# Scores of the later attention layers as three products of split operands, with the queries held by token tile

## The chip, the cores and the metric

One core of one Trainium2 chip runs the whole program. The metric is the device time of one execution in microseconds (us); the time before is the median of three executions, 2535.29 us (2534.57 to 2535.4).

## What is computed

Two transformer blocks in a row on 256 tokens of width 1024, batch 1. The first has two layers with a second stream of 256 context tokens (differential and neighbourhood attention, then grouped attention over context and tokens). The second has four layers: attention (layer 0), a linear recurrence (1), latent attention (2), attention (3), and in each a cross attention to a memory and a feed-forward part with a short convolution. The change is in the attention of layers 0 and 3 of the second block; the same function also serves the last layer of the first block. Cut to its core, the reference of layers 0 and 3 is

```python
qkv = x @ w_qkv
q, k, v = jnp.split(qkv, ...)
q = apply_rope_2(q.reshape(bsz, s, A_HEADS, A_HEAD_DIM), cos, sin)
k = apply_rope_2(k.reshape(bsz, s, A_KV_HEADS, A_HEAD_DIM), cos, sin)
...
scores = jnp.einsum('bnqhgd,bnkhd->bnhgqk', qb, kb).astype(jnp.float32) * (A_HEAD_DIM ** -0.5)
scores = jnp.where(valid[None, :, None, None], scores, NEG)
probs = jax.nn.softmax(jnp.concatenate([scores, sink], axis=-1), axis=-1)[..., :-1]
out = jnp.einsum('bnhgqk,bnkhd->bnqhgd', probs.astype(v.dtype), vb)
return out.reshape(bsz, s, A_HEADS * A_HEAD_DIM) @ w_o
```

with 16 query heads of width 64, 4 key heads and blocks of 128 tokens: a query of the first token tile sees the 128 keys of its tile, one of the second tile sees 256 keys, through a mask.

## The kernel before, in words

All activations and weights are float32. Large products are made with operands split in two: `split` (L154 to L161) writes a high part, rounded to the type float32r, on ACT, and then on DVE the rest, the low part; `mm3` (L137 to L141) issues three matmuls into the same bank: high by high (L139), one high by the other's low (L140), low by high (L141). `weights` (L125 to L135) loads 1 MB of weights and splits it in four pieces of 512 columns on ACT (L133) and DVE (L134). A product of plain float32 operands is one matmul call, which the trace shows as two records, each with its own weight load.

`gqa` (L675 to L787) makes one attention layer. In layers 0 and 3 (no `cT`) it projects keys and values (`rows`), applies the rotation (`rope`, DVE, last instruction L276), transposes the keys on TensorE (L165) into one PSUM bank `t` and copies them into the tile `kT`, float32, 2 x 256 columns. `query(J)` projects half of the heads, rotates and transposes each token tile (four transposes into bank `t`) and copies it with the factor 0.125 into its columns of `qT`, a float32 tile of 4 x 256 columns in two buffers. `attend` then calls `quad_attn` (L790 to L828) for each half J (2), token tile t (2) and pair of head columns g (2): 8 calls in a layer, 16 in the two layers. A call makes the scores of four heads: for i and j in 0, 1 one matmul (L804) with 64 rows, j being the half of the partitions (0 to 63 or 64 to 127), into the bank `s[j]`:

```python
for i in range(2):
    for j in range(2):
        hs = slice(HD * j, HD * (j + 1))
        nc.tensor.matmul(s[j][:, i * nk : (i + 1) * nk], qT[hs, g + i, t * P : (t + 1) * P], kT[hs, J, :nk],
                         start=True, stop=True)
```

`nk` is 128 for t = 0 and 256 for t = 1. Mask and maximum follow on DVE (L808), the exponentials on ACT (L812), the division on DVE (L818), then four transposes into bank `t` (L165), a copy on ACT (L824), and the products with the values (L826). Bank `t` is a single buffer; `s` has two.

In the last layer of the first block (`cT` given) keys and queries are already split; `pair_attn` (L420 to L462) issues the three products of one half of the partitions, then the three of the other, with 512 columns each.

`copy` (L143 to L152) puts a copy on DVE (L148, L150) or on ACT (L152) by a toggle, `flip`, that every call turns: in layers 0 and 3 the values (2 calls), `kT` (1), `qT` (4) and the 12 copies of `quad_attn`, which turn the toggle too though they are fixed to ACT. The latent attention of layer 2 uses `copy` for its operands (`kr`, `mv`, `qr`, `qk`, `mpt`).

What sets the order: the source lists the instructions, and a scheduler in the tile framework orders them for each engine when the program is built, so that PE works on other matmuls (the next projection, the output projection of `project`, L831 to L861) between the steps of an attention. Semaphores hold an instruction until its operands are there. Each layer's tiles live in a pool of its own (`atM0`, `atM3`).

Of the kernel before, what the change touches and what calls it, by code (L numbers as in the profile page):

```python
# [19 lines left out]
P = 128  # L20
D = 1024
S = 256
# [36 lines left out]
class Net:  # L59
# [615 lines left out]
    def gqa(self, xT, w_qkv, kind, sink, cT=None):  # L675

        nc = self.nc
        T = lambda n, shape, b=1: self.at.tile(shape, F32, tag=n, name=n, bufs=b)
        TT = lambda n, shape, b=1: [self.at.tile(shape, F32R, tag=n + c, name=n + c, bufs=b) for c in "hl"]
        nkt = 4 if cT is not None else 2  # L680
        kT, v = (T if cT is None else TT)("kT", [P, 2, nkt * P]), T("gv", [P, nkt, S])
        oT = self.pair("T", S)
        kv = [self.bank("a") for _ in range(2)]
        if cT is not None:
# [1 line left out]
        def rows(ps, w, kh, t, x=xT):  # L686
            for k in range(4):
                kk = 4 * kh + k
                self.mm3(ps[t], [z[:, kk, t * P : (t + 1) * P] for z in x], [z[:, k, :] for z in w],
                         kk == 0, kk == KD - 1)  # L690
# [26 lines left out]
        pt = self.bank("t")  # L717
# [5 lines left out]
                o = J * S + t * P  # L723
                self.transpose(pt[:, o : o + P], rk[:, J * P : (J + 1) * P])
        pt = pt.rearrange("p (f t) -> p f t", f=2)
        if cT is None:
            self.copy(kT, pt)
        else:
            self.split(pt, *(x[:, :, :S] for x in kT))

        def query(J):
            ps = [self.bank("a") for _ in range(2)]
            for kh in range(2):
                w = [x.rearrange("p (k n) -> p k n", k=4) for x in self.weights(w_qkv[1 + J, kh])]
                for t in range(2):
                    rows(ps, w, kh, t)
            qT = (T if cT is None else TT)("qT", [P, 4, S], 2)
            for t in range(2):
                rq = self.wk.tile([P, 512], F32, tag="w", bufs=4, name="rq")
                self.rope(rq, ps[t], 512, kind, t)  # L740
                pt = self.bank("t")
                for g in range(4):
                    self.transpose(pt[:, g * P : (g + 1) * P], rq[:, g * P : (g + 1) * P])
                pt, ts = pt.rearrange("p (g q) -> p g q", g=4), slice(t * P, (t + 1) * P)
                if cT is None:
                    self.copy(qT[:, :, ts], pt, 0.125)
                else:
                    self.split(pt, *(x[:, :, ts] for x in qT), scale=0.125)
            return qT

        def attend(J, qT, ts=(0, 1)):
            hs = lambda j: slice(HD * j, HD * (j + 1))
            for t in ts:
                ops = self.bank("o")
                ts = slice(t * P, (t + 1) * P)
                if cT is not None:
                    for g in range(4):
                        if t == 0:
                            bias = lambda j: (P, self.cst[:, C_MLE0 : C_MLE0 + P])
                        else:  # L760
                            bias = lambda j: (0, self.cst[:, C_GE0 : C_GE0 + P])
                        self.pair_attn(
                            lambda j: [x[hs(j), g, ts] for x in qT],
                            lambda j: [x[hs(j), J, :] for x in kT],
                            512,
                            lambda j, kb: v[:, kb, (2 * J + j) * HD : (2 * J + j + 1) * HD],
                            ops[:, g * P : (g + 1) * P],
                            bias=bias,
                            sink=sink + 8 * J + 2 * g,
                        )  # L770
                        self.fill(1 if J else g % 2)
                else:
                    for g in range(0, 4, 2):
                        self.quad_attn(qT, kT, v, J, t, g, ops, sink + 8 * J + 2 * g)
                self.split(ops.rearrange("p (g q) -> p g q", g=4), *(o[:, 4 * J : 4 * J + 4, ts] for o in oT))

        q0 = query(0)
        self.update()
        attend(0, q0)
        q1 = query(1)  # L780
        if cT is not None:
            attend(1, q1)
            yield oT, [0, 1, 2, 3]
        else:
            attend(1, q1, (0,))
            yield oT, [0, 1]
            attend(1, q1, (1,))  # L787
            yield oT, [2, 3]

    def quad_attn(self, qT, kT, v, J, t, g, ops, sink):  # L790

        nc = self.nc
        nk = (t + 1) * P
# [6 lines left out]
        s = [self.bank("s") for _ in range(2)]  # L800
        for i in range(2):
            for j in range(2):
                hs = slice(HD * j, HD * (j + 1))
                nc.tensor.matmul(s[j][:, i * nk : (i + 1) * nk], qT[hs, g + i, t * P : (t + 1) * P], kT[hs, J, :nk],  # L804
                                 start=True, stop=True)
        for h in range(4):
            j, i = divmod(h, 2)
            nc.vector.tensor_tensor_reduce(out=e[:, h, :nk], in0=s[j][:, i * nk : (i + 1) * nk], in1=mask, scale=1.0,  # L808
# [10 lines left out]
        for kb in range(t + 1):  # L819
            ps = self.bank("t")  # L820
            pt = self.at.tile([P, 512], F32, tag="pt", name="pt")
# [3 lines left out]
            for j in range(2):  # L825
                nc.tensor.matmul(ops[HD * j : HD * (j + 1), g * P : (g + 2) * P],  # L826
                                 v[:, kb, (2 * J + j) * HD : (2 * J + j + 1) * HD], pt[:, j * S : (j + 1) * S],
                                 start=kb == 0, stop=kb == t, skip_group_check=True)  # L828
# [821 lines left out]
```

## Time and profile before

| | |
|---|---|
| median of three executions | 2535.29 us |
| the profiled execution, its own time | 2532.55 us |
| its span, first to last instruction | 2530.8 us |
| PE busy | 2468.3 us (98%) |
| DVE busy | 1701.7 us (67%) |
| ACT busy | 1214.9 us (48%) |
| granted TensorE clock, mean | 0.996 |

PE is the engine of the matmuls, PEld its weight loads (they overlap PE), DVE the vector engine, ACT the scalar engine. A matmul's record is longer than its share of the engine, since matmuls are pipelined: what one costs is read from start to start. Columns of the timeline: start and duration in us, engine, line, operation, out<-in, shape, how many were merged, and in brackets the idle time before it and what ended it. In the two attention layers the scores lie at 1153 to 1191 us and at 2207 to 2247 us of the span.

### The profile page before, as it was taken

Reading aid. Unit: us, or ns where it says so; the run is one execution under the profiler, and the core shown is the slowest. Engines: PE = TensorE matmul, PEld = TensorE weight load, DVE = VectorE, ACT = ScalarE, POOL = GpSimd, SP = SyncE. Lnnn points to the kernel's source line nnn. Section 1 sums busy time; section 2 is a strip of 40 time slices with the busy share of each in tenths; the row PEclk is TensorE's granted clock in tenths of the full one; section 3 lists DMA queues with packets and bytes.
Section 4 is the critical chain, followed back from the end, with each engine's and each line's share of the span. In section 5 each row is a group of like instructions: output and inputs, shape, how many; then the busy total and the mean of one; then the engine's idle time right before and its main releaser. Section 6 shows DMA issues by size and latency. Waiting matters only on the chain.

```text
span 2530.8 us, 39873 instructions
## 1 busy us (share of the span) xinstructions
PE 2468.3 (98%) x15706; PEld 2094.4 (83%) x15706; DVE 1701.7 (67%) x3602; ACT 1214.9 (48%) x2630; POOL 130.6 (5%) x172
## 2 busy tenths in 40 slices
PE   7999999999999999999999999999999999999998
PEld 5957668777788679986899988999878999869998
DVE  5463674343448765568787789677877777986777
ACT  4242353222235445446455665465555455564664
POOL 2000001111100000000000010000000000000000
PEclk9999999999999999999999999999999999999999
DMA  9415324343223546543545545355345455433643
GB/s 391 171 48 214 124 77 178 138 156 142 89 84 134 212 152 223 192 167 133 183 167 189 189 150 219 125 212 195 135 154 184 149 200 184 169 147 123 236 176 116
DMA packets 63708, 419.31 MB, mean 166 GB/s; under 512 B 7440, under 2 KB 7696, under 8 KB 16928
## 3 DMA queue, kind: packets, MB, share of 16 engines
q1 hardware_dynamic: 62240, 412.56, 45.3%
q0 software_dynamic: 1280, 4.20, 0.5%
q8 instruction: 123, 2.02, 0.3%
q14 instruction: 65, 0.53, 0.1%
HBM read 411.45 MB, written 5.28 MB: 165 GB/s over the span
## 4 chain that ended last, share of the span: by engine, by line
PE 85%; DVE 8%; ACT 3%; issue 1%; POOL 1%; DMA 1%; POOLq 0%; DVEq 0%; ACTq 0%
PE banka L139 9%; PE banka L140 9%; PE banka L141 9%; PE banks L139 6%; PE banks L141 6%; PE banks L140 6%; PE bankb L141 5%; PE bankb L140 5%; PE bankb L139 5%; PE bankt L165 3%; PE banko L141 2%; PE banko L139 2%; PE banko L140 2%; DVE wlo L134 2%; PE bankt L141 2%; PE bankt L140 2%
## 5 line engine op out<-in xcount | busy, mean ns | idle before, releaser
L134 DVE TENSOR_TENSOR wlo<-raw,whi 128x512 fp32r<-128x512 f32 (+1 forms) x1184 | 783.4, 689 | 290.9 <-ACT whi L133 288.1
L133 ACT ACTIVATE whi<-raw 128x512 fp32r<-128x512 f32 (+1 forms) x1184 | 662.7, 620 | 641.0 <-issue 175.4
L141 PE MATMUL banks<-Th,wlo 128*128 128x256 f32 x880 | 249.5, 284 | 3.0 <-DVE wlo L134 3.0
L139 PE MATMUL banks<-Th,whi 128*128 128x256 f32 x880 | 249.3, 283 | 0.6 <-DVE uf L250 0.6
L140 PE MATMUL banks<-Tl,whi 128*128 128x256 f32 x880 | 249.1, 283 | 0.0
L141 PEld LDWEIGHTS banks<-Th,wlo 128*128 128x128 f32 x880 | 168.8, 192 | 4.1 <-DVE wlo L134 4.1
L139 PEld LDWEIGHTS banks<-Th,whi 128*128 128x128 f32 x880 | 168.8, 192 | 1.7 <-issue 0.7
L140 PEld LDWEIGHTS banks<-Tl,whi 128*128 128x128 f32 x880 | 168.8, 192 | 0.8
L139 PE MATMUL banka<-whi,Th 128*128 128x512 f32 (+1 forms) x304 | 122.2, 404 | 2.6 <-ACT Th L157 2.1
L140 PE MATMUL banka<-wlo,Th 128*128 128x512 f32 (+1 forms) x304 | 120.0, 397 | 2.1 <-DVE wlo L134 2.0
L141 PE MATMUL banko<-Th,wlo 128*128 128x256 f32 x424 | 120.9, 285 | 1.1 <-DVE wlo L134 1.1
L655 DVE TENSOR_TENSOR sg<-sg,bankb 128x512 f32<-128x512 f32 x22 | 15.1, 688 | 158.3 <-PE bankb L141 158.3
L139 PE MATMUL bankt<-Th,whi 128*128 128x256 f32 x424 | 120.3, 284 | 0.0
L139 PE MATMUL banko<-Th,whi 128*128 128x256 f32 x424 | 120.1, 283 | 0.0
L141 PE MATMUL bankt<-Th,wlo 128*128 128x256 f32 x424 | 120.0, 283 | 0.0
L140 PE MATMUL bankt<-Tl,whi 128*128 128x256 f32 x424 | 120.0, 283 | 0.0
L140 PE MATMUL banko<-Tl,whi 128*128 128x256 f32 x424 | 119.9, 283 | 0.0
L141 PE MATMUL banka<-whi,Tl 128*128 128x512 f32 (+1 forms) x304 | 117.7, 394 | 0.3 <-DVE Tl L158 0.3
L139 PE MATMUL bankb<-Th,whi 128*128 128x256 f32 (+1 forms) x344 | 115.0, 335 | 0.0
L141 PE MATMUL bankb<-Th,wlo 128*128 128x256 f32 (+1 forms) x344 | 114.8, 334 | 0.0
L140 PE MATMUL bankb<-Tl,whi 128*128 128x256 f32 (+1 forms) x344 | 114.2, 332 | 0.0
L157 ACT ACTIVATE hh<-hf 128x256 fp32r<-128x256 f32 x110 | 45.7, 415 | 135.1 <-DVE hf L955 134.6
(489 smaller groups left out, 6356.2 us busy)
## 6 DMA issues: line engine op xcount, KB each, us to landing
raw<-in_f_w_up_dram SPq DMA_DIRECT2D x88, 1024.0 KB, 4.8
raw<-in_ffn_w_dram SPq DMA_DIRECT2D x66, 1024.0 KB, 4.9
adaw<-in_ada_w_dram SPq DMA_DIRECT2D x48, 1024.0 KB, 4.8
raw<-in_f_w_down_dram SPq DMA_DIRECT2D x44, 1024.0 KB, 5.0
raw<-in_x_w_q_dram SPq DMA_DIRECT2D x16, 1024.0 KB, 4.8
raw<-in_x_w_o_dram SPq DMA_DIRECT2D x16, 1024.0 KB, 5.7
raw<-in_w_in_ab_dram SPq DMA_DIRECT2D x12, 1024.0 KB, 5.8
raw<-in_a_w_qkv_dram SPq DMA_DIRECT2D x12, 1024.0 KB, 4.9
```

The source lines that it names most:

```text
L133: nc.scalar.activation(hi[:, a:b], r[:, a:b], AF.Copy)
L134: nc.vector.tensor_tensor(lo[:, a:b], r[:, a:b], hi[:, a:b].bitcast(F32), op=ALU.subtract)
L139: mm(out, l[0], r[0], start=start, stop=False)
L140: mm(out, l[0], r[1], start=False, stop=False)
L141: mm(out, l[1], r[0], start=False, stop=stop)
L157: nc.scalar.activation(hi, src, AF.Copy)
L165: self.nc.tensor.transpose(out, src, self.ident[:k, :k])
L655: nc.vector.tensor_tensor(sg, sg, ps[1], op=ALU.mult)
```

## The change

In layers 0 and 3 `kT` becomes a pair (high and low, float32r), written by `split` instead of `copy`. `qT` becomes one pair for each token tile, 4 x 128 columns, in three buffers for layers 0 and 3 and in four for the first block's last layer, written by `split` with the factor 0.125. `quad_attn` takes the pair of its token tile and calls `mm3` in place of the one float32 matmul. Five calls of `copy` leave each of layers 0 and 3.

```diff
@@ -678,7 +678,7 @@
-        kT, v = (T if cT is None else TT)("kT", [P, 2, nkt * P]), T("gv", [P, nkt, S])
+        kT, v = TT("kT", [P, 2, nkt * P]), T("gv", [P, nkt, S])
@@ -723,10 +723,7 @@
-        if cT is None:
-            self.copy(kT, pt)
-        else:
-            self.split(pt, *(x[:, :, :S] for x in kT))
+        self.split(pt, *(x[:, :, :S] for x in kT))
@@ -734,18 +731,14 @@
-            qT = (T if cT is None else TT)("qT", [P, 4, S], 2)
+            qT = [TT("qT", [P, 4, P], 3 if cT is None else 4) for _ in range(2)]
...
-                pt, ts = pt.rearrange("p (g q) -> p g q", g=4), slice(t * P, (t + 1) * P)
-                if cT is None:
-                    self.copy(qT[:, :, ts], pt, 0.125)
-                else:
-                    self.split(pt, *(x[:, :, ts] for x in qT), scale=0.125)
+                self.split(pt.rearrange("p (g q) -> p g q", g=4), *qT[t], scale=0.125)
@@ -760,7 +753,7 @@
-                            lambda j: [x[hs(j), g, ts] for x in qT],
+                            lambda j: [x[hs(j), g, :] for x in qT[t]],
@@ -771,7 +764,7 @@
-                        self.quad_attn(qT, kT, v, J, t, g, ops, sink + 8 * J + 2 * g)
+                        self.quad_attn(qT[t], kT, v, J, t, g, ops, sink + 8 * J + 2 * g)
@@ -801,8 +794,8 @@
-                nc.tensor.matmul(s[j][:, i * nk : (i + 1) * nk], qT[hs, g + i, t * P : (t + 1) * P], kT[hs, J, :nk],
-                                 start=True, stop=True)
+                self.mm3(s[j][:, i * nk : (i + 1) * nk], [x[hs, g + i, :] for x in qT], [x[hs, J, :nk] for x in kT],
+                         True, True)
```

## Rows read from the trace of the kernel before

**Rows 1.** The page: busy time by engine, and shares of the chain that ended last.

```profile
PE 2468.3 (98%) x15706; PEld 2094.4 (83%) x15706; DVE 1701.7 (67%) x3602; ACT 1214.9 (48%) x2630; POOL 130.6 (5%) x172
...
PE 85%; DVE 8%; ACT 3%; issue 1%; POOL 1%; DMA 1%; POOLq 0%; DVEq 0%; ACTq 0%
```

**Rows 2.** Windows: stretch, its length, busy us by engine; both attentions, and a full stretch of DVE.

```profile
1150.00:1205.00 55.00, 55.00 (x295) 35.85 (x295) 43.39 (x169) 35.47 (x107) 0.00 (x0) 1.00 0.27 96
2205.00:2260.00 55.00, 54.41 (x294) 35.84 (x293) 44.69 (x172) 35.67 (x107) 0.74 (x2) 1.00 0.30 110
...
2210.00:2220.00 10.00, 10.00 (x56) 6.62 (x55) 9.82 (x44) 7.77 (x25) 0.00 (x0) 1.00 0.57 211
```

**Rows 3.** Groups by line and shape: the score matmuls (busy us, mean ns).

```profile
L804 PE MATMUL banks<-kT,qT 64*128 64x256 f32 x64 | 14.5, 413 | 0.0
L804 PE MATMUL banks<-kT,qT 64*128 64x128 f32 x64 | 6.7, 299 | 0.0
```

**Rows 4.** Timeline of PE: scores of 128 columns, in one stretch and divided.

```profile
1152.44 0.39 PE L141 MATMUL banka<-whi,Tl 128*128 128x512 f32 x1
1152.67 0.40 PE L139 MATMUL banka<-whi,Th 128*128 128x512 f32 x1
1153.00 0.71 PE L804 MATMUL banks<-kT,qT 64*128 64x128 f32 x8
1153.64 0.50 PE L140 MATMUL banka<-wlo,Th 128*128 128x512 f32 x1
...
2209.00 0.49 PE L804 MATMUL banks<-kT,qT 64*128 64x128 f32 x2
```

**Rows 5.** Timeline of PE: scores of 256 columns, in one stretch and divided.

```profile
1156.82 1.14 PE L804 MATMUL banks<-kT,qT 64*128 64x256 f32 x8
...
1161.74 1.13 PE L804 MATMUL banks<-kT,qT 64*128 64x256 f32 x4
...
1163.16 0.70 PE L804 MATMUL banks<-kT,qT 64*128 64x256 f32 x2
```

**Rows 6.** Timeline of PE: split products of 256 columns, one after another.

```profile
1881.14 0.28 PE L139 MATMUL banks<-cqh,whi 128*128 128x256 f32 x1
1881.26 0.28 PE L140 MATMUL banks<-cql,whi 128*128 128x256 f32 x1
```

**Rows 7.** Transposes of 128 columns: four in the timeline, then their group by shape.

```profile
1154.44 0.60 PE L165 MATMUL bankt<-cst,rq 128*128 128x128 f32 x4
...
L165 PE MATMUL bankt<-cst,rq 128*128 128x128 f32 x64 | 10.0, 278 | 2.2 <-DVE rq L276 2.2
```

**Rows 8.** Timeline of PE in the first block's last layer: one pair of split scores.

```profile
870.53 0.50 PE L139 MATMUL banks<-kTh,qTh 64*128 64x512 f32 x1
870.68 0.50 PE L139 MATMUL bankb<-kTh,qTh 64*128 64x512 f32 x1
870.87 0.39 PE L140 MATMUL banks<-kTl,qTh 64*128 64x512 f32 x1
...
871.10 0.39 PE L141 MATMUL banks<-kTh,qTl 64*128 64x512 f32 x1
```

**Rows 9.** Tiles: the copies that go, and the split's two halves (min/median/max ns).

```profile
L152 ACT ACTIVATE qT<-bankt x4: 586/597/599, 1152.2 to 2236.1; 128x512 f32<-128x512 f32 x4
L150 DVE TENSOR_SCALAR qT<-bankt x4: 682/692/692, 1155.1 to 2234.6; 128x512 f32<-128x512 f32 x4
...
L160 ACT ACTIVATE qTh<-bankt x4: 577/589/600, 798.6 to 867.6; 128x512 fp32r<-128x512 f32 x4
L161 DVE SCALAR_TENSOR_TENSOR qTl<-bankt,qTh x4: 681/681/683, 799.4 to 868.4; 128x512 fp32r<-128x512 f32 x4
```

**Rows 10.** Timeline of PE behind the first attention: output projection, first and last of its end.

```profile
1203.99 0.50 PE L139 MATMUL bankb<-whi,Th 128*128 128x512 f32 x1
...
1212.95 0.39 PE L141 MATMUL bankb<-whi,Tl 128*128 128x512 f32 x1
```

**Rows 11.** Timeline of PE in layer 2, latent attention: the longest wait.

```profile
1858.50 0.63 PE L165 MATMUL bankt<-cst,rq 128*128 128x128 f32 x4 [1.57 <-DVE rq L276]
```

## The prediction

> **What bounds the kernel now.** I began with the page: PE is busy for 98% of the span, and 85% of the chain that ended last is PE [rows 1]. An average over the span does not settle one stage, so I took windows over the two attentions that change. From 1150 to 1205 us PE is busy all 55 us, from 2205 to 2260 us 54.4 of 55, both at the full granted clock, which is the higher of TensorE's two levels (2.4 GHz) [rows 2]. There PE's own time is the time: a step that occupies PE for longer is paid, one that delays another engine is paid only once PE has no other matmul to do. PE does have some: the scheduler has set projection matmuls between the steps of an attention, and behind the first attention the output projection still runs for 9 us (1203.99 to 1212.95) [rows 10]. DVE is the engine to watch beside it, with 44.7 of 55 us in the second attention and 9.8 of 10 us at its fullest [rows 2].
>
> What can be touched is small. The groups by shape give all score matmuls of the two layers: 14.5 us busy for 256 columns and 6.7 us for 128 columns, 21.2 us or 0.84% of the span [rows 3]. About 0.2% (5.1 us) is what a measurement of this kernel can tell from no change, so a quarter of all this must come or go to be seen.
>
> **The change part by part.** *What a score costs now.* 32 matmuls have 128 columns and 32 have 256; each shows as two records. The timeline lets the price of a record be read by differences. One matmul of 128 columns (two records) takes 0.49 us, a whole call (eight records) 0.71 us [rows 4]: the two halves of the partitions run side by side, so a call is four records deep, and two more in depth cost 0.22 us, 0.11 us each. With 256 columns two records take 0.70 us and four of one half 1.13 us [rows 5], so 0.215 us each.
>
> *What it costs after.* Each matmul becomes three split products, so a half is six deep, not four. For 256 columns the trace has the price: split products start 0.12 us apart [rows 6]. That these have 128 rows and the scores 64 I take as no difference, since with 512 columns one half's products of 64 rows follow each other in 0.23 us (870.87 to 871.10) [rows 8], as those of 128 rows do (1152.44 to 1152.67) [rows 4]. Side by side a call goes from 4 x 0.215 = 0.86 to 6 x 0.12 = 0.72 us, -0.14; where the scheduler has divided a call and one half runs after the other, each matmul gains 0.43 - 0.36 = 0.07, -0.28 for the call's four. Both forms stand in the trace [rows 5].
>
> For 128 columns no split product stands in the trace. Each loads 128 columns of weights anew, and so do the transposes, which start (0.60 - 0.28) / 3 = 0.107 us apart [rows 7]; float32 records of this width also take 0.11 [rows 4]. I take 0.11, since the weight load is the same size. The bound below is half a 256-column product, 0.06 (if only columns counted); the bound above is the whole float32 matmul it replaces, two records, 0.22. At 0.11 a call goes from 4 x 0.11 to 6 x 0.11, +0.22.
>
> By the Trainium skill (TensorE: Matmul & The Clock Gate, section Back-to-back issue gap) 128 columns at full clock would take 56 ns, an estimate near the lower bound, and the whole sum below would come to -0.5 us; no row here shows a split product that short.
>
> *Do the halves still run side by side?* The code issues three products of one half, then three of the other. In the first block's last layer it does the same, and there the second half starts at 870.68, 0.15 us after the first at 870.53 and before the first half's second product at 870.87 [rows 8]. So they overlap, with about 0.10 us more offset than the float32 pairs have. I add 0.10 to each call that runs in one stretch.
>
> The Trainium skill says on the same page (section The mechanism) that matmuls start and end strictly in program order and only weight loads move ahead. By that rule only one product in three would overlap, a call would be nine deep, and the sum would be +4.1 us. The alternating starts in the row do not fit it if the program holds the order of the code.
>
> *PE's sum.* 128 columns: 8 calls x (0.22 + 0.10) = +2.6 us. 256 columns: I count four of the eight calls as side by side (-0.14 + 0.10 = -0.04) and four as divided (-0.28), -1.3 us. Each further division of a call costs PE 0.2 us, 0.10 on the way in (0.33 in place of 0.23 between the starts at 1152.67 and 1153.00) and 0.11 on the way out (0.50 in place of 0.39) [rows 4]. There are 25 stretches for 16 calls now (the first at 1153.00); with three times the instructions I count two more, +0.4 us.
>
> *The splits.* Eight query copies (four of 0.60 us on ACT, four of 0.69 on DVE) and two key copies become ten high parts of 0.59 on ACT and ten low parts of 0.68 on DVE [rows 9]: five more instructions on each engine, 2.9 and 3.4 us. Each key or query tile is ready some 0.7 us later, and bank `t`, a single buffer, is held as much longer, so the transposes behind it wait. PE's cover is the projections [rows 10]. I count +0.2 us for a cover that DVE's fullness pierces once; if the cover were gone everywhere it would be 10 x 0.68 = 6.8 us, and no gain is possible here, since nothing leaves the wait. The third query buffer costs nothing: the fourth tile reuses the first one's, whose readers, the first calls of 128 columns, are done when those of 256 begin at 1156.82 [rows 5], before the second half's queries are projected. For the first block's last layer the four smaller buffers hold the same bytes and I count zero, with a new order of up to 0.5 us either way.
>
> *A side effect.* Five calls of `copy` fewer is an odd number, so the toggle comes out turned over, and in layer 2 every free copy changes its engine. PE waits there for DVE (1.57 us before the transposes at 1858.50) [rows 11]; the first query copy moves to DVE next to that wait, the second away. I count zero, with one copy, 0.7 us, either way.
>
> **Sum:** 2.6 - 1.3 + 0.4 + 0.2 = +1.9 us. The profiled execution took 2532.55 us, its span 2530.8 and 1.75 around it; +1.9 makes 2534.45. The median of the runs is 2.74 above that execution, so the forecast for the median is 2537.2 us, +0.08%: no difference that can be measured.
>
> **The rivals.** *Slower, by the narrow product:* a split product of 128 columns takes as long as the float32 matmul, 0.22 us. Then a call of that width goes from 0.44 to 1.32 plus 0.10, 8 x 0.98 = 7.8 in place of 2.6, the sum is +7.1, the time 2542.4 us. It decides above 0.18 us a product (48 more in depth by 0.07 make the 3.2 us to the bound). For it: no row has one to contradict it. Against it: the weight loads set 0.11 in two kinds of rows [rows 4, 7]. Chance 0.17.
>
> *Slower, by the low halves:* the second attention's DVE is so full [rows 2] that every low part delays PE and nothing covers it: +1.7 + 6.8 = +8.5, 2543.8 us. It decides once over half of the ten are bare. Against it: PE waited 0.6 us in that stretch of 55 [rows 2]. Chance 0.10.
>
> *Faster, by whole calls:* with operands ready tile by tile, the scheduler no longer divides the calls. All eight of 256 columns would then take 0.23 + 5 x 0.12 + 0.28 + 0.15 = 1.26 us (a first step of 0.12 and the 0.11 by which first steps are longer, 870.53 to 870.87 against 0.23 [rows 8]; five more; the last record; the offset) where they average 14.5 / 8 = 1.81 [rows 3], -4.4; nine divisions fewer give back what lies outside those records, 0.11 each, -1.0; and 128 columns at 0.06 cost nothing more than now. With the splits' +0.2 that is -5.2, 2530.1 us. Against it: it needs all three at once. Chance 0.13.
>
> **How the numbers follow.** The forecast, within 0.2% of 2535.29 (2530.2 to 2540.4), has 0.60. Faster by over 0.2% has the 0.13 of its rival; slower has 0.17 + 0.10 = 0.27. The range is 2530.0 to 2544.0: below it lies most of what the faster case could add, above it only mixtures of the two slower ones.
>
> **What would show each step.** PE's score groups: 96 products of 128 and 96 of 256 columns; starts 0.11 apart in one half for 128, 0.12 for 256; halves alternating. Their busy time should end near 22 us. Ten high and ten low parts of 0.59 and 0.68. PE busy in the two windows as full as now. Layer 2 with `mpt` on ACT and `qk` on DVE. I am wrong if starts of 128 columns lie 0.2 apart, if PE waits for `qTl` or bank `t` by more than 3 us in all, or if the difference lies outside the two attentions.

## The result, and the profile after

The change is slower: the median of its runs is 2548.18 us (2546.07 to 2551.29) against 2535.35 for the kernel before, a ratio of 1.0052 with a 95% interval of 1.0035 to 1.0069. The profiled execution took 2549.86 us, its span is 2548.1: 17.3 more than the span shown of before. These 17.3 are 12.8 between the medians, 2.8 by which the profiled execution of before lies under its median and 1.7 by which this one lies above its own; the shifts below are those of one execution each. Lines of `quad_attn` behind the scores have moved by 7 (the maxima are L801, the division L811); the split products run on L139 to L141.

The page of the changed kernel, busy time by engine and shares of the chain that ended last, answers to [rows 1]:

```profile
PE 2478.5 (97%) x15770; PEld 2104.7 (83%) x15770; DVE 1706.7 (67%) x3607; ACT 1217.5 (48%) x2635; POOL 130.4 (5%) x172
...
PE 83%; DVE 10%; ACT 3%; issue 1%; DMA 1%; POOL 1%; POOLq 0%; DVEq 0%; ACTq 0%
```

PE is busy for 10.2 us more and idle for 7.1 more. Where, the windows say (behind the length: busy us of PE, PEld, DVE, ACT and POOL, the granted clock, DMA share, GB/s; the second attention now begins 8 us later):

```profile
1150.00:1205.00 55.00, 52.98 (x297) 36.19 (x296) 43.59 (x168) 34.90 (x106) 0.00 (x0) 1.00 0.28 96
2213.00:2268.00 55.00, 51.51 (x282) 35.83 (x280) 43.24 (x164) 33.94 (x104) 0.00 (x0) 0.94 0.30 104
2222.60:2229.40 6.80, 6.80 (x22) 5.23 (x23) 3.31 (x19) 2.34 (x10) 0.00 (x0) 0.50 0.45 161
```

PE, idle for 0 and 0.6 us of these stretches before [rows 2], is now idle for 2.0 and 3.5 us, and for 6.8 us of the second stretch TensorE is granted half its clock (0.50, the level of 1.2 GHz). Matching the matmuls that both kernels have, those behind the first attention come 5.7 us later than those ahead of it, those behind the second 8.1 us. These 13.8 us are the change; the rest is 1.2 us behind the first attention, a net 1.1 in layer 2 and 1.5 behind the second. Part of it goes with stretches at half clock that differ between executions (layer 2 has one of 3.4 us here and none in the execution of before).

The groups by line and shape, for [rows 3]:

```profile
L139 PE MATMUL banks<-kTh,qTh 64*128 64x256 f32 x32 | 9.9, 361 | 1.2 <-ACT stat L807 1.1
...
L141 PE MATMUL banks<-kTh,qTl 64*128 64x256 f32 x32 | 8.8, 310 | 0.0
L140 PE MATMUL banks<-kTl,qTh 64*128 64x256 f32 x32 | 8.2, 298 | 0.0
L139 PE MATMUL banks<-kTh,qTh 64*128 64x128 f32 x32 | 6.5, 309 | 1.7 <-DVE stat L801 1.7
L141 PE MATMUL banks<-kTh,qTl 64*128 64x128 f32 x32 | 5.8, 285 | 0.0
L140 PE MATMUL banks<-kTl,qTh 64*128 64x128 f32 x32 | 5.7, 273 | 0.0
```

The scores are no longer free of idle time: they stand for `stat`, the maxima that DVE takes from a call's banks. The 1.1 us that the first row puts down to ACT (L807) is one wait, ahead of the products at 2222.54, and it ends as much with DVE:

```profile
2222.10 0.28 DVE L801 CUSTOM_DVE_ANT_0 e<-banks,cst 128x128 f32<-128x128 f32 x1
2222.28 0.19 ACT L807 ACTIVATE stat<-stat 128x4 f32<-128x4 f32 x1
```

Both end within 0.1 us of each other. The scores read nothing of what L807 writes, and the maximum is the second of the two that hold their first bank, so I count this wait as DVE's. One narrow call (128 columns) in the timeline of PE:

```profile
1157.17 0.33 PE L139 MATMUL banks<-kTh,qTh 64*128 64x128 f32 x1 [0.27 <-DVE stat L801]
1157.33 0.27 PE L140 MATMUL banks<-kTl,qTh 64*128 64x128 f32 x1
1157.44 0.28 PE L141 MATMUL banks<-kTh,qTl 64*128 64x128 f32 x1
1157.59 0.34 PE L139 MATMUL banks<-kTh,qTh 64*128 64x128 f32 x2
...
1157.97 0.27 PE L139 MATMUL banks<-kTh,qTh 64*128 64x128 f32 x1
...
1158.20 0.27 PE L141 MATMUL banks<-kTh,qTl 64*128 64x128 f32 x1
```

The first bank comes free at 1157.17, and three products run alone; the second bank comes free 0.42 us later, and only from there do two products start together. The call takes 1.03 us from first start to last where eight float32 records took 0.44 to 0.53. The second part of that wait is not idle time in any view, since one half of PE is at work. DVE's timeline shows why the bank is late:

```profile
1153.60 0.68 DVE L276 TENSOR_TENSOR rq<-rq,t 128x512 f32<-128x512 f32 x1
1154.20 1.89 DVE L134 TENSOR_TENSOR wlo<-raw,whi 128x512 fp32r<-128x512 f32 x3
1156.01 0.68 DVE L161 SCALAR_TENSOR_TENSOR qTl<-bankt,qTh 128x512 fp32r<-128x512 f32 x1
1156.61 0.28 DVE L801 CUSTOM_DVE_ANT_0 e<-banks,cst 128x128 f32<-128x128 f32 x1
```

The first maximum of the first call starts 3.47 us after the call's first product (1153.14), behind three low parts of weights and the low part of the second query tile. The first two scores had their last products at 1153.94, so most of this is DVE's queue; the call's other two follow at 1155.27, behind the transposes of the second tile. In the kernel before the lag was 1.08 us (the first product at 1153.00 [rows 4]):

```profile
1154.08 0.28 DVE L808 CUSTOM_DVE_ANT_0 e<-banks,cst 128x128 f32<-128x128 f32 x1
```

It was 0.75 in the three other attention halves; now it is 2.6 to 3.6 in all four. The waits of PE in both attentions together (1150 to 1212, then 2212 to 2272), where before had one, of 0.4 us:

```profile
PE banks L139 <- DVE stat L801: 1.1, 2, 0.8
PE bankt L165 <- DVE e L811: 0.7, 1, 0.7
...
PE bankt L165 <- DVE e L811: 1.5, 2, 1.2
PE banks L139 <- ACT stat L807: 1.1, 1, 1.1
PE banks L139 <- DVE stat L801: 0.6, 1, 0.6
```

By starts, with the usual step of 0.33 us between a 512-column product and the next shape taken off, the waits ahead of calls and transposes are 2.3 us in the first attention and 3.3 in the second, and the late second banks inside four calls make 4 x 0.42 = 1.7. That is 7.3 of the 13.8 us: some 5.3 for the banks of the scores, and 2.0 ahead of transposes, for `e`, the exponentials that DVE has divided (L811). The 6.8 us at half clock cost at most half of that, 3.4 (an estimate). What is left, 3.1 or more, is products, turns between shapes and splits; it is found by difference and not measured.

### The profile page after: what moved, and what is told of

The parts are those of the page before. It is cut to its first block, busy times and chain, and to the rows that moved or that the text cites. A ratio compares the mean times of both kernels' runs of the same rounds, so it can differ in the third digit from the quotient of the medians.

```text
span 2548.1 us, 40010 instructions
## 1 busy us (share of the span) xinstructions
PE 2478.5 (97%) x15770; PEld 2104.7 (83%) x15770; DVE 1706.7 (67%) x3607; ACT 1217.5 (48%) x2635; POOL 130.4 (5%) x172
## 4 chain that ended last, share of the span: by engine, by line
PE 83%; DVE 10%; ACT 3%; issue 1%; DMA 1%; POOL 1%; POOLq 0%; DVEq 0%; ACTq 0%
PE banka L139 9%; PE banka L140 9%; PE banka L141 9%; PE banks L139 6%; PE banks L141 6%; PE banks L140 6%; PE bankb L141 5%; PE bankb L140 4%; PE bankb L139 4%; PE bankt L165 3%; DVE wlo L134 2%; PE banko L141 2%; PE banko L139 2%; PE banko L140 2%; PE bankt L141 2%; PE bankt L140 2%
## 5 line engine op out<-in xcount | busy, mean ns | idle before, releaser
L141 PE MATMUL banks<-Th,wlo 128*128 128x256 f32 x880 | 249.5, 284 | 3.1 <-DVE wlo L134 3.1
L139 PE MATMUL banks<-Th,whi 128*128 128x256 f32 x880 | 249.3, 283 | 0.6 <-DVE uf L250 0.6
L141 PEld LDWEIGHTS banks<-Th,wlo 128*128 128x128 f32 x880 | 168.8, 192 | 4.1 <-DVE wlo L134 4.1
L139 PEld LDWEIGHTS banks<-Th,whi 128*128 128x128 f32 x880 | 168.8, 192 | 1.7 <-issue 0.8
L139 PE MATMUL banka<-whi,Th 128*128 128x512 f32 (+1 forms) x304 | 122.5, 405 | 2.4 <-ACT Th L157 2.2
L141 PE MATMUL banko<-Th,wlo 128*128 128x256 f32 x424 | 120.9, 285 | 2.6 <-DVE wlo L134 2.5
L139 PE MATMUL bankt<-Th,whi 128*128 128x256 f32 x424 | 120.3, 284 | 0.0
L139 PE MATMUL banko<-Th,whi 128*128 128x256 f32 x424 | 120.1, 283 | 0.0
L141 PE MATMUL bankt<-Th,wlo 128*128 128x256 f32 x424 | 120.0, 283 | 0.0
L141 PE MATMUL banka<-whi,Tl 128*128 128x512 f32 (+1 forms) x304 | 119.2, 398 | 0.3 <-DVE Tl L158 0.3
L139 PE MATMUL bankb<-Th,whi 128*128 128x256 f32 (+1 forms) x344 | 115.0, 335 | 0.0
L141 PE MATMUL bankb<-Th,wlo 128*128 128x256 f32 (+1 forms) x344 | 114.7, 334 | 0.0
```

What stands on the lines that cost most here:

```text
L139: mm(out, l[0], r[0], start=start, stop=False)
L141: mm(out, l[1], r[0], start=False, stop=stop)
```

## The experiments

Eighteen kernels, in four groups. The table has each one's median, its ratio to the kernel before with the 95% interval, and from its profile the shift over the first and the second attention (found as above, against the trace of before) and the time at half clock within the two.

| kernel | us | ratio | first | second | half clock |
|---|---|---|---|---|---|
| change | 2548.2 | 1.0052 (1.0035 to 1.0069) | 5.7 | 8.1 | 6.8 |
| halves alternate | 2549.8 | 1.0065 (1.0052 to 1.0077) | 7.3 | 8.7 | 13.6 |
| third product of high parts | 2551.5 | 1.0070 (1.0057 to 1.0083) | 8.3 | 9.7 | 10.2 |
| no low queries | 2551.4 | 1.0063 (1.0050 to 1.0077) | 5.9 | 9.4 | 13.7 |
| toggle turned back | 2550.3 | 1.0062 (1.0048 to 1.0076) | 7.1 | 8.0 | 6.8 |
| before, toggle turned | 2535.0 | 1.0006 (0.9997 to 1.0015) | 0.0 | -0.5 | 0 |
| before, tiles alone | 2535.5 | 1.0004 (0.9995 to 1.0013) | 0.1 | 0.0 | 0 |
| float32 of high parts | 2539.7 | 1.0020 (1.0011 to 1.0030) | 1.6 | 1.2 | 0 |
| wide calls split alone | 2541.3 | 1.0022 (1.0011 to 1.0032) | 2.7 | 2.9 | 0 |
| narrow calls split alone | 2553.0 | 1.0076 (1.0062 to 1.0089) | 7.8 | 9.4 | 6.8 |
| mixed | 2538.5 | 1.0017 (1.0009 to 1.0026) | 1.7 | 4.8 | 3.4 |
| maxima first | 2546.3 | 1.0048 (1.0035 to 1.0060) | 7.1 | 3.7 | 6.9 |
| four banks | 2547.4 | 1.0052 (1.0040 to 1.0064) | 5.8 | 7.6 | 20.5 |
| four banks, alternate | 2546.3 | 1.0055 (1.0042 to 1.0069) | 5.4 | 7.9 | 20.4 |
| maxima first, four banks | 2542.3 | 1.0039 (1.0024 to 1.0053) | 3.9 | 4.2 | 6.8 |
| weights on GpSimd | 2563.3 | 1.0115 (1.0102 to 1.0129) | 13.0 | 16.0 | 20.5 |
| before, weights on GpSimd | 2560.7 | 1.0101 (1.0086 to 1.0117) | 13.9 | 13.9 | 13.6 |
| before, four banks | 2530.8 | 0.9987 (0.9979 to 0.9996) | -0.4 | -1.7 | 0 |
| before, tiles, four banks | 2528.7 | 0.9982 (0.9973 to 0.9991) | -1.9 | -1.6 | 0 |

Where a kernel has a stretch at half clock just ahead of the first attention (halves alternate, third product, toggle turned back, weights on GpSimd in both kernels, before with four banks), up to 1.7 us of its first shift may belong to that (3.4 for before with weights on GpSimd).

### What it is not: order of the halves, toggle, tiles, low halves

**Halves alternate.**

```diff
-            for j in range(2):
-                hs = slice(HD * j, HD * (j + 1))
-                self.mm3(s[j][:, i * nk : (i + 1) * nk], [x[hs, g + i, :] for x in qT], [x[hs, J, :nk] for x in kT],
-                         True, True)
+            for p, (l, r) in enumerate(((0, 0), (0, 1), (1, 0))):
+                for j in range(2):
+                    hs = slice(HD * j, HD * (j + 1))
+                    nc.tensor.matmul(s[j][:, i * nk : (i + 1) * nk], qT[l][hs, g + i, :], kT[r][hs, J, :nk],
+                                     start=p == 0, stop=p == 2)
```

> The changed kernel, with the same 192 split products in another order: for each score pair the first product of one half of the partitions, then of the other, and so on. Three theories. Order (TensorE starts matmuls in the order of the program, so three of one half in a row let only the third overlap the other half): a call of 12 products of 128 columns falls from 1.03 us between its first and last start to 0.16 + 5 x 0.11 = 0.71 or less, of 256 columns from 1.03 to about 0.8; 16 calls by 0.25 to 0.35 give 4 to 5.6 us back, and the median goes from 2548.2 to 2543 or 2544. Waits (PE stands for the scores' banks, for e and for bank t, and the clock drops behind the longest wait): the runs of twelve shorten or not, the median stays at 2546 to 2551, since the waits stay. Split products of two halves do not overlap at all: the runs of twelve stay at 1.0 or grow to 1.3 us.

The median did not fall, and a call of twelve still takes 1.03 us. The timeline of PE in this kernel shows what holds it:

```profile
1189.96 0.33 PE L798 MATMUL banks<-kTh,qTh 64*128 64x128 f32 x1 [0.35 <-DVE stat L802]
1190.13 0.27 PE L798 MATMUL banks<-kTl,qTh 64*128 64x128 f32 x1
1190.38 0.33 PE L798 MATMUL banks<-kTh,qTh 64*128 64x128 f32 x1
1190.39 0.32 PE L798 MATMUL banks<-kTh,qTl 64*128 64x128 f32 x1
...
1190.99 0.27 PE L798 MATMUL banks<-kTh,qTl 64*128 64x128 f32 x1
```

The other half's first product starts 0.42 us after the first one's, as in the changed kernel, because its bank is that much later; from 1190.38 on the call takes 0.61 us, six deep. The order theory falls.

**Toggle**, turned over in the kernel before, and turned back in the changed one, each time at the end of an attention:

```diff
             attend(1, q1, (1,))
+            self.flip ^= 1
             yield oT, [2, 3]
```

> The kernel before with its toggle turned over once at the end of each of the two attentions, so that the free copies of the layers between them run on the engines that the change gives them; nothing else. If the turned toggle costs, as the shift of 2 us within layer 2 lets one suspect: 2537 to 2538.5. If that shift belongs to something else: 2534.8 to 2536.2, no difference.

> The changed kernel with its toggle turned back at the end of each of the two attentions, so that the layers between them have the engines of the kernel before for their copies. If the turned toggle costs: about 2 us less than 2548.2, or up to 4 if the stretch at half clock behind 1867 us goes with it. If it does not: 2546 to 2551 as now.

Neither shows a difference that can be measured (1.0006, interval over 1; and 2550.3 beside 2548.2). The profiled execution with the toggle turned is 3.5 us later over layer 2, where it has a stretch at half clock; its eleven runs together do not bear that out.

**Tiles alone**, in the kernel before (float32, the same copies and matmuls):

```diff
-            qT = (T if cT is None else TT)("qT", [P, 4, S], 2)
+            qT = [(T if cT is None else TT)("qT", [P, 4, P], 3 if cT is None else 4) for _ in range(2)]
```

> The kernel before with one part of the change alone: its float32 queries are kept by token tile, in three buffers each (four in the first block's last layer), with the same copies and the same matmuls. Float32 on the high parts stood 5.8 us above before. If the tiles make a good part of that (a new order of the instructions): 2536 to 2539. If the splits, the toggle and the clock make it: 2533 to 2536.

No difference that can be measured (0.9995 to 1.0013), as the second theory has it: tiles and buffers by themselves cost nothing here.

**Third product of high parts, then no low queries at all.**

```diff
+                hl = [(qT[x][hs, g + i, :], kT[y][hs, J, :nk]) for x, y in ((0, 0), (0, 1), (0, 1))]
+                for p, (l, r) in enumerate(hl):
+                    nc.tensor.matmul(s[j][:, i * nk : (i + 1) * nk], l, r, start=p == 0, stop=p == 2)
...
+                if cT is None:
+                    nc.scalar.activation(qT[t][0], pt.rearrange("p (g q) -> p g q", g=4), AF.Identity, scale=0.125)
```

The first kernel has the first part of the edit, the second both.

> The changed kernel, but the third product of each score is the second one over again (high part of the query by low part of the key), so no score reads the query's low part, which is still computed; as many products, as much work on DVE. If what costs is that a score has to wait for a low half that is 0.7 us later: 2537 to 2541. If it is DVE's order: the built order has two weight splits ahead of the first maximum where the changed kernel has three and a low half, so the waits shrink by about half, 2542 to 2546. If it is the products: 2546 to 2551.

> As the run with the third product of high parts, and the query's low parts are not computed either: eight instructions of 0.68 us less on DVE, and bank t is free as early as before the change. If DVE's load or bank t's longer hold costs: 2537 to 2541. If it is DVE's order: three weight splits still stand ahead of the first maxima in the built order, so 2541 to 2546. If it is the products: 2546 to 2551.

Both are as slow as the change. Without any low part of a query, DVE's timeline still has, behind a first product at 1153.39:

```profile
1153.86 0.68 DVE L276 TENSOR_TENSOR rq<-rq,t 128x512 f32<-128x512 f32 x1
1154.46 1.89 DVE L134 TENSOR_TENSOR wlo<-raw,whi 128x512 fp32r<-128x512 f32 x3
1156.27 0.29 DVE L805 CUSTOM_DVE_ANT_0 e<-banks,cst 128x128 f32<-128x128 f32 x1
```

So neither the latency of the queries' low halves, nor their 0.68 us each on DVE, nor bank `t` held longer for them is what costs. The three weight splits ahead of the maxima stay in this half. In the four halves the lag is 2.9, 2.2, 2.1 and 0.9 us, shorter than in the change, and yet nothing is gained; TensorE spends 13.7 us at half clock in place of 6.8. The lag alone does not set the loss.

### Which part: the narrow calls

```diff
-                self.mm3(s[j][:, i * nk : (i + 1) * nk], [x[hs, g + i, :] for x in qT], [x[hs, J, :nk] for x in kT],
-                         True, True)
+                nc.tensor.matmul(s[j][:, i * nk : (i + 1) * nk], qT[0][hs, g + i, :].bitcast(F32),
+                                 kT[0][hs, J, :nk].bitcast(F32), start=True, stop=True)
```

This stands everywhere in the first kernel, for `t == 0` (128 columns) in the second, for `t == 1` (256 columns) in the third.

> The changed kernel with its query tiles, its three buffers, its splits and its copies as they are, but each score is one float32 matmul of the high parts, as the kernel before has one of the whole values (the low parts are still computed and nothing reads them, so the scores lose them). Order theory, or any theory by which the products themselves are dear: PE busy falls back by 5 us or more to about 2470 and the median to 2536 to 2541. Theory of the splits (the later low halves, bank t held longer, the tiles, the turned toggle): the median stays above 2544. The part of the 12.8 us that stays is what splits, buffers and toggle cost together.

> The changed kernel, but the calls of 128 columns are one float32 matmul of the high parts (these scores lose the low parts); the calls of 256 columns keep their three products, and all splits are computed. Theory of the order on DVE: the first calls no longer wait for a low half, the maxima stand ahead of the weight splits again, and the median is 2537 to 2541, like the run with float32 everywhere (2539.7). Theory of the products: only the 128-column part of their cost goes, 3.7 us by the strides, so 2545 to 2546.

> The counterpart of the run with wide calls alone: the calls of 128 columns are three products, those of 256 columns one float32 matmul of the high parts (these scores lose the low parts). If the parts add (float32 of high parts everywhere 5.8 us above before, narrow products 6.1 more, wide products 0.9 more): 5.8 + 6.1 = 11.9 above before, 2545 to 2548. If the narrow products are harmless by themselves and only both together fill DVE or TensorE: 2538 to 2542.

With float32 in the narrow calls most of the loss is gone (2539.7 and 2541.3; 0.20 and 0.22% in place of 0.52). What stays in the first of them comes without any split product of scores; of its 0.20% (0.11 to 0.30, some 5 us) the two shifts hold 2.8 us, and where the rest lies is open. In these two the first maximum starts 0.74 to 1.19 us after the call's first product, as before the change; for the wide calls alone, with the first product at 1154.20:

```profile
1154.07 0.68 DVE L161 SCALAR_TENSOR_TENSOR qTl<-bankt,qTh 128x512 fp32r<-128x512 f32 x1
1154.66 0.68 DVE L276 TENSOR_TENSOR rq<-rq,t 128x512 f32<-128x512 f32 x1
1155.26 0.29 DVE L808 CUSTOM_DVE_ANT_0 e<-banks,cst 128x128 f32<-128x128 f32 x1
```

With narrow calls split alone the lag is 2.9 to 3.6 us and the median 2553.0. So the narrow calls carry most of the loss. The parts do not add as expected, though: narrow calls alone are 18.7 us above their own runs of before, more than the whole change's 12.8, although the two intervals still meet.

**Mixed**: first tile's queries and first 128 keys whole, wide calls split and alternating.

```diff
+            kF = T("kF", [P, 2, P])
+            self.copy(kF, pt[:, :, :P])
...
+            qT = [T("qF", [P, 4, P], 2) if cT is None and t == 0 else
+                  TT("qT", [P, 4, P], 2 if cT is None else 4) for t in range(2)]
```

> A mixture of both kernels that keeps all of the precision: the first token tile's queries and the first 128 keys stay whole (float32, one matmul a score of 128 columns), the second tile's calls of 256 columns are three split products, issued alternately for the two halves; the first tile's query copies are as before the change and the keys have one copy more. By the strides so far the 256-column products save about 1 us an attention where nothing waits; the 128-column ones cost nothing then. Theory of the order on DVE: 2533 to 2537, no measurable difference from before, perhaps 1 us faster. Theory that any split product costs: 2540 and more.

2538.5, an interval above 1: the wide products give nothing back on the whole, and the expectation was 1.5 us too low.

### What TensorE waits for

**Maxima first**: the second tile's split is traced behind the first call's maxima, and the next weight splits are queued behind the last of these.

```diff
+                if first and t == 0:
+                    first(qT)
...
+                with self.tc.issue_after(self.pin):
+                    nc.vector.tensor_tensor(lo[:, a:b], r[:, a:b], hi[:, a:b].bitcast(F32), op=ALU.subtract)
```

> The changed kernel with DVE's order of the kernel before forced upon it at the start of each attention half: the second query tile's transposes and split are traced behind the first call's scores and maxima, and the weight splits that follow are queued behind its last maximum. All 192 split products, all splits and the turned toggle stay. Theory of the order on DVE (in the changed kernel the first call's four maxima stand behind three weight splits and the second tile's low half, 3.5 us after the call's first product where it was 1.1, so the next call stands for its banks): the waits for the scores' banks and for e go, TensorE's stretch at half clock behind 2222 us goes with them, and the median falls from about 2549 by 6 to 10 us, to 2539 to 2543. Theory of the products (192 split products are what costs): 2546 to 2551 as now.

2546.3, within the range of the second theory, and its interval (1.0035 to 1.0060) lies for the most part in the change's: no gain that can be told, and the expected 6 to 10 us did not come. The lag falls to 1.4 to 1.5 us, the waits for the first banks go, and the next call stands instead. PE in this kernel:

```profile
1157.91 0.40 PE L145 MATMUL banka<-whi,Th 128*128 128x512 f32 x1
1159.60 0.91 PE L145 MATMUL banks<-kTh,qTh 64*128 64x256 f32 x2 [1.29 <-DVE stat L824]
```

Other waits are new: in the two attentions PE stands 1.4 us for `wlo`, the weights' low parts that the forced order makes late, and 1.1 for `qTh`. The edit moves the wait, and so it cannot settle whether DVE's order is the cause.

**Four banks**, in the changed kernel, with alternating halves, and with the maxima first:

```diff
-        s = [self.bank("s") for _ in range(2)]
+        s = [self.bank("s" if J and t else "sb") for _ in range(2)]
```

> The changed kernel, with the scores of all but the last tile's calls taking their banks from four in turn (the pair s and the pair b, which nothing else uses there) and not from two, so that a call need not stand for the maxima of the one just ahead. Theory of the bank waits (TensorE stands for the scores' banks because DVE comes late to the maxima): the single products at the head of the runs of twelve go (0.42 us in each of four calls, 1.7), the waits ahead of them go (about 4 us), and the median falls by 4 to 7 us to 2542 to 2545. If the wait only moves to the next thing that DVE owes (e, for the transposes): 2546 to 2550.

> The changed kernel with four banks for the scores and its products issued alternately for the two halves. With four banks alone nothing waited ahead of the runs of narrow products, but 41 score products followed each other within 5.4 us and the clock stood at half behind them (10 us in the two attentions, some 5 us lost), so the median hardly fell. Theory that the dense run of narrow products draws the clock down: side by side the same 41 products take less time, but they are as many and as narrow, so the stretches at half clock stay and the median is 2544 to 2548. Theory that a run's length in time does it: shorter runs, fewer stretches at half clock, 2538 to 2543.

> Both at once: DVE's order forced as in the run with the maxima first, and four banks for the scores. The run with the maxima first was left with 2 x 1.3 us for the banks of the first call of 256 columns. Theory of the bank waits: those go too, and with them the stretch at half clock behind the first: 2539 to 2543. Theory of the products: 2545 or more.

Four banks alone move the wait on to the third call, and something else takes over. PE and then the windows of that kernel:

```profile
1152.49 0.32 PE L139 MATMUL banks<-kTh,qTh 64*128 64x128 f32 x1
1152.50 0.32 PE L139 MATMUL bankb<-kTh,qTh 64*128 64x128 f32 x1
1152.65 0.27 PE L140 MATMUL banks<-kTl,qTh 64*128 64x128 f32 x1
1152.66 0.27 PE L140 MATMUL bankb<-kTl,qTh 64*128 64x128 f32 x1
1152.77 0.27 PE L141 MATMUL banks<-kTh,qTl 64*128 64x128 f32 x1
...
1154.76 0.35 PE L139 MATMUL banks<-kTh,qTh 64*128 64x256 f32 x1 [1.04 <-DVE stat L801]
```

```profile
1147.00:1152.00 5.00, 4.58 (x26) 3.25 (x25) 4.73 (x11) 2.68 (x5) 0.00 (x0) 1.00 0.55 210
1152.50:1157.50 5.00, 3.96 (x40) 3.60 (x40) 4.45 (x24) 3.64 (x12) 0.00 (x0) 0.81 0.18 26
...
1158.20:1162.00 3.80, 3.80 (x12) 3.06 (x12) 1.39 (x9) 1.52 (x7) 0.00 (x0) 0.50 0.43 179
```

41 score products follow each other from 1152.49, with one wait among them, and the clock falls to half while they run and stays there behind them; the two attentions spend 20.5 us at half clock (not 10, as the expectation for alternating halves says of this kernel), which can cost up to 10 of their 13.4 us. Alternating halves change nothing in this (20.4 us). With the maxima first as well, the median is 2542.3: the best of the changed kernel's versions, its two shifts 8.1 us in place of 13.8 with as much time at half clock. Its interval (1.0024 to 1.0053) still overlaps the change's. Nor is it the bank waits alone that went. PE in its first attention:

```profile
PE banks L145 <- ACT qTh L166: 1.1, 2, 0.6
PE banks L147 <- DVE qTl L167: 0.8, 3, 0.4
PE bankt L171 <- DVE e L835: 0.8, 1, 0.8
PE banka L146 <- DVE wlo L137: 0.8, 2, 0.5
...
PE banks L145 <- DVE stat L824: 0.2, 1, 0.2
```

For the score banks 0.2 us is left, but PE stands for other operands: it is idle for 7.0 us in the two attentions, 5.5 in the change. What fell as well is the number of stretches that the scores are divided into, from 35 to 14; at the prediction's 0.2 us each that is some 4 us (an estimate) of the 5.7 by which the shifts fell. No run keeps the two apart.

**Weights on GpSimd**, in the changed kernel and in the one before:

```diff
-            nc.vector.tensor_tensor(lo[:, a:b], r[:, a:b], hi[:, a:b].bitcast(F32), op=ALU.subtract)
+            e = nc.gpsimd if self.share else nc.vector
+            e.tensor_tensor(lo[:, a:b], r[:, a:b], hi[:, a:b].bitcast(F32), op=ALU.subtract)
```

> The changed kernel; while the two attentions run, the low parts of the weights are subtracted on GpSimd and not on DVE (in its place such a slice may take 1.35 us, as GpSimd's additions of 128x512 do, where DVE takes 0.69). Theory that DVE's queue is what TensorE waits for: the three weight splits ahead of the first maxima are gone, the waits for the scores' banks and for e, 7.4 us by the strides, fall to 2 or less, and unless TensorE waits for GpSimd's slower slices instead, the median is 2539 to 2544. If the order on TensorE itself sets the waits (a call is queued too close behind the one whose banks it needs, whatever DVE does): the waits for banks stay, 2546 to 2551.

> The control: the kernel before with the same weight splits on GpSimd. It hardly waits for DVE in the attentions (0.4 us), so little can be gained: 2531 to 2536; where GpSimd's slices come too late for the projections, it is slower, and the run of the changed kernel has to be read against this.

They are 29 and 26 us slower than before, so as an answer to the first question the pair is spoiled: one of these splits takes 1.41 us on GpSimd and 0.68 on DVE, and the control loses as much. Against each other they are 2.7 us apart where the change costs 12.8. In the changed kernel with this edit the waits for the score banks fall from 1.1 and 1.7 us to 0.5 in each attention, although the second tile's low part still stands ahead of the maxima and the lag stays at 2.4 us or more. That fits a loss that arises in DVE's queue; but in stretches so much slower other waits can hide it, and it is no proof.

### A version ahead of both

> The kernel before with the same four banks for the scores. It did not stand for a score's bank, so the theory of the bank waits gives no difference: 2533 to 2536. If four banks help or hurt by another way (a new order of the instructions), it shows here, and the run of the changed kernel with four banks is to be read against this one.

> The kernel before with four banks for its scores (2530.8, ahead of before by 0.13%) and with the query tiles of the change, still float32. The tiles alone made no difference, so 2530 to 2533, the same lead; if four banks only gained by a chance order of the instructions, the tiles may turn it over: 2533 to 2536.

The kernel before with four banks for its scores, the same line of code as above, is ahead by 0.13%, and with the query tiles of the change by 0.18% (2528.7 us), both with the whole interval below 1. The windows of the second, for [rows 2]:

```profile
1150.00:1205.00 55.00, 54.48 (x305) 36.48 (x304) 45.44 (x173) 35.26 (x107) 0.42 (x2) 1.00 0.29 99
2205.00:2260.00 55.00, 54.16 (x300) 36.63 (x298) 46.09 (x175) 36.11 (x109) 0.74 (x2) 1.00 0.32 118
```

More matmuls fit into the same 55 us at the full clock (305 and 300 in place of 295 and 294). I had expected no difference, since before did not stand for these banks: what the banks gave was a denser order, not a wait removed. The scores run in 14 stretches in both kernels where before has 25; at the prediction's 0.2 us a division that is 2.2 us (an estimate) of the 2.1 and 3.5 by which the two attentions together got shorter.

## Why the prediction was wrong

The forecast was no difference (2537.2, range 2530.0 to 2544.0); it came out at 2548.2, above the range.

- **Price of a split product: right.** Starts of 128 columns lie 0.11 us apart (1157.33, 1157.44), of 256 columns 0.12. The slower rival by the narrow product (0.22) falls. The 56 ns that the prediction takes from the Trainium skill (TensorE: Matmul & The Clock Gate, section Back-to-back issue gap) is that section's gap for a matmul by itself; for a stream of weight loads and matmuls it gives about 81 ns at 128 columns. These rows are above both. The sum of -0.5 us beside it belongs to the lower bound of 0.06; by 56 ns it would be -0.7.
- **Halves side by side, six deep: right where both banks are free.** In the kernel with four banks the built order is three products of one half, then three of the other, and the two halves still start 0.01 us apart (1152.49, 1152.50), closer than the offset of 0.10 that I added. The rule of the Trainium skill (TensorE: Matmul & The Clock Gate, section The mechanism), strict program order, does not fit these rows: one half's first product (1152.50) starts ahead of the other half's second (1152.65), which stands before it in the program. By the prediction's own terms that rule's sum would have been +4.8 us, not +4.1. That calls were nine deep all the same came from the second bank.
- **Divisions:** 35 stretches where I counted 27; the eight more are some 1.6 us at the forecast's 0.2 each. They belong to the 3.1 us of products, turns and splits, against +1.9 forecast: a small miss.
- **The step that failed is "I count +0.2 us for a cover that DVE's fullness pierces once".** The waits on DVE were 7.3 us in its place. I had asked who waits for the low halves and bank `t`; the wait that came is, for some 5.3 of the 7.3 us, for the two banks `s`, which the text never priced: the next call's scores stand until DVE has taken the maxima of the last. [rows 2] showed DVE at 9.8 of 10 us just there, and that was the warning. The rival "slower by the low halves" (2543.8, +8.5 us) came nearest to the measured 12.8, with the wrong cause: without low halves of the queries the kernel is no faster.
- **Missing from the sum: the clock.** [rows 2] had 1.00 in both attentions and I took it as given. 6.8 us at half clock, at most 3.4 us, came in.
- **Toggle and tiles at zero: right**, by runs of each alone. The faster rival, by whole calls, falls: more divisions, not fewer.

Shown, then: most of the loss comes with the narrow split calls, and the trace of the change puts 7.3 us of it on waits for DVE and up to 3.4 on the clock. Not shown is that DVE's order causes the loss: with the order forced and the banks doubled the two shifts fall from 13.8 to 8.1 us, but the number of stretches falls with them, and the medians do not part clearly. Open: why the scheduler sets weight splits and the second tile's low part ahead of the maxima when the calls are split products (with the same tiles and float32 in the narrow calls it does not), whether the narrow calls split alone are slower than all calls split, and if so why; and what the splits cost without split products (some 5 us by the ratio, 2.8 in the shifts, where +0.2 was forecast).

## What to carry to other kernels

Where a call needs a bank that another engine has yet to read, price the round trip: scores, the reader's place in its own queue, next scores. Here calls that are only 0.2 us dearer came with a queue that the scheduler had filled with other work first, and the trace then shows the wait and not the products as the larger part. Before work is swapped, count the buffers in that round: in the medians, doubling the score banks gave more to the kernel before than any form of the split gave.

## What the runs showed of the hardware that was not expected

- Split products of 64 rows from the two halves of the partitions run in pairs: both halves start within 0.01 us, the next pair 0.16 us and the one after it 0.12 us later (1152.49 to 1152.77 above).
- The granted clock fell where scores were narrow split products. In the two attentions it stayed at 1.00 in all kernels with narrow calls in float32 but two, the mixed one (3.4 us at half clock) and the one with late weights on GpSimd (13.6). All eleven with narrow split calls spent 6.8 to 20.5 us at half clock there, each in one profiled execution. In the kernel with four banks the fall came behind narrow products, a wait of 1.04 us and wide products (PE busy 3.96 of 5.00 us, granted 0.81, then 0.50). What of these brings it about is not shown.
